# A hybrid diffusion step on one core: RWKV chunk steps with merged elementwise instructions, a planner that counts changes of first partition, and decays formed earlier

## The chip, the cores and the metric

The kernel runs on one core of a Trainium2 chip. The metric is the device time of one execution in microseconds (us). Of the core's engines five appear here: TensorE (PE; its weight loads are PEld), VectorE (DVE), ScalarE (ACT), GpSimd (POOL) and SyncE (SP, which issues all DMAs).

## The reference

Two layers work on 128 context tokens and 512 latent tokens of width 2048. Each layer normalizes and modulates its input, multiplies it by one input projection (2048 by 7056), runs three mixers on groups of the columns (gated linear attention with 6 heads, a chunked spatial MLP with 4 groups, and RWKV-7 with 12 heads), gates each and multiplies by one output projection (2048 by 2048). What the change touches is RWKV-7, a recurrence of a 64 by 64 state per head, run forwards and backwards:

```
def _rwkv7_scan(r, w, k, v, a, b, s0):
    def step(s, inp):
        r_t, w_t, k_t, v_t, a_t, b_t = inp
        sa = jnp.einsum('bhvk,bhk->bhv', s, a_t)
        s = (s * w_t[:, :, None, :] + sa[..., None] * b_t[:, :, None, :]
             + v_t[..., None] * k_t[:, :, None, :])
        return s, jnp.einsum('bhvk,bhk->bhv', s, r_t)
...
decay = jnp.exp(-jnp.exp(w_log)).reshape(N_DIR, B, L, RW_HEADS, RW_HEAD_DIM)
...
k_dir = k[None] * (1.0 + (iclr - 1.0) * lw['rw_ka'].astype(f32).reshape(hn))
b_dir = kk[None] * iclr
y_f, s_f = _rwkv7_scan(r, decay[0], k_dir[0], v, -kk, b_dir[0], s0[:, 0])
y_b, s_b = _rwkv7_scan(flip(r), flip(decay[1]), flip(k_dir[1]), flip(v), flip(-kk), flip(b_dir[1]), s0[:, 1])
```

## The kernel before

**The large products.** Every weight block is loaded in float32 (tile `raw`), split into a rounded part `whi` (ACT or DVE) and a rest `wlo` (DVE), and multiplied with the split activations `hi` and `lo` in three passes. For the input projection the 640 tokens are two halves of 320, so PE's rows read `pz<-hi,whi`, `pz<-lo,whi`, `pz<-hi,wlo` with 320 columns. The output projection has 512 columns. The modulation weights (`raw`, `csp`) are 32-wide products.

**RWKV.** `rwkv_quad` (line 895) takes four heads (two pairs, index `j`, two heads of a pair on partitions 0 to 63 and 64 to 127, index `q`) and one half of 320 tokens in each direction (index `d`), five chunks of 64. There are three quads with two halves each, six such halves in a layer and twelve in the kernel, each in this order:

- decays (lines 906 to 988), four times, once for each `j` and `d`: products with the low-rank weights (`pl<-ta,w2a`), tanh, a scan and three exponentials, then products by VectorE on one half of the partitions at a time into `ag` and `bk`, then `pl<-ag,bk` on PE, masked back into `gb` and `ag`, and transposes (`pl<-kc,bk`) into `ken`.
- inversion (lines 990 to 1050): a triangular system of 32 by 32 blocks, 31 pairs of VectorE instructions on `svu` and `lk`, and small products.
- five chunk steps (from line 1075). Each is a chain: ACT scales the state into `s0p` (eight instructions of 64 by 64); PE multiplies (`pl<-svu,ag`, 16 products into PSUM tiles X and Y); DVE copies `xs`; PE multiplies (`pl<-xs,gb`); DVE copies into `svu` (four instructions of 64 by 128); PE multiplies (`pl<-svu,ken` and `pl<-svu,gb`); DVE forms the next state with eight instructions of 64 by 64, each state times decay plus `s0p`, into `svu`, into `scar` for the next half or into `so` for the output; ACT copies the outputs into `ag`.

`rwkv_end` (line 1194) later normalizes and gates a pair's result (`pl<-kc,tw`, `pl<-tw,kc`).

**What sets the order.** The code is only recorded. `Scheduler.run` (line 300) then plays all instructions through a list of costs (`price`, line 215) and writes a fixed order for each engine; on the chip every engine follows its order and waits by semaphores. An instruction's priority is its place in the recording less a boost. RWKV has one boost, weight loads ten, the projections none: projections are what PE does while the chain of RWKV is not ready. Priorities also order who gets a buffer first; the PSUM pool `pl` has three banks for X, Y, the low-rank products and the rest of RWKV. In costs, DVE and ACT instructions follow one another with no gap:

```
            o.cost = 0.066 + 0.062 * ex + n * (0.00104 if two or ps else 0.00052)
...
                o.start = s
                t[e] = s + c
```

`layer` (line 1518) lists steps of the projections and of the other mixers; after each it records one step of RWKV (`RSTEP = 1`), once three steps of the pairs it needs are recorded. `rwkv_all` (line 1178) runs the halves one after the other: a half is recorded wholly before the next begins.

## Time and profile before

| | |
|---|---|
| median of 3 runs | 3136.03 us (3131.77 to 3136.59) |
| the profiled execution's own time | 3133.72 us |
| its span, first to last instruction | 3131.9 us |
| busy: PE, PEld, DVE, ACT, POOL | 2898.4, 2559.2, 2150.3, 1197.9, 105.0 us |
| mean granted clock of TensorE | 0.974 of full speed |

Busy time is the time in which at least one instruction of the engine runs. PE's matmuls overlap one another, so PE can be busy and still be slowed a little. A wait in the trace is idle time of an engine, put down to the instruction that released it. All instructions carry line 462 (473 in the changed program), where the order is written out; rows are told apart by the names of their tiles, and `tsm` is in these rows the small tiles, the decays `p5` among them.

### The profile page before, as it was taken

The numbers are of one execution on the slowest core, as the hardware profiler recorded it, in microseconds if no ns is written. First come the engines' busy times: TensorE is split into PE (matmuls) and PEld (weight loads), VectorE is DVE, ScalarE is ACT, GpSimd is POOL, SyncE is SP. The second block draws the span as 40 slices with busy tenths as digits, with TensorE's granted clock in tenths as the row PEclk, the third lists the DMA queues.
The fourth block names the chain that finished last, engine by engine and source line by source line (L and its number), as shares of the span: only waits on it lengthen the run. The fifth ranks groups of instructions, "written<-read, shape, count | busy, mean of one in ns | idle before, by whom it ended". The sixth has DMA issues, their size and how long they took to land. (4 is left out here: it accounts for less than half of the span.)

```text
span 3131.9 us, 64037 instructions
## 1 busy us (share of the span) xinstructions
PE 2898.4 (93%) x24531; PEld 2559.2 (82%) x24531; DVE 2150.3 (69%) x5200; ACT 1197.9 (38%) x2641; POOL 105.0 (3%) x281
## 2 busy tenths in 40 slices
PE   4899999999899999999999999999989998998998
PEld 2688688788888878988879877888879887998786
DVE  3357686785776867655576668769778696866557
ACT  3252643435343354431015336344534335434001
POOL 0000000000000000000000000000000000000000
PEclk9899899999999999999999999999999999999999
DMA  9856375565555645465463654635534453437335
GB/s 307 261 157 170 92 203 142 160 182 155 148 142 161 182 118 150 124 206 161 125 201 104 176 140 139 186 95 137 156 98 121 107 155 96 103 99 228 114 111 194
DMA packets 672154, 478.13 MB, mean 153 GB/s; under 512 B 188596, under 2 KB 606088, under 8 KB 671848
## 3 DMA queue, kind: packets, MB, share of 16 engines
q1 hardware_dynamic: 671848, 474.04, 53.3%
q8 instruction: 194, 3.18, 0.4%
q14 instruction: 112, 0.92, 0.1%
HBM read 393.63 MB, written 79.59 MB: 151 GB/s over the span
## 5 line engine op out<-in xcount | busy, mean ns | idle before, releaser
L462 PE MATMUL pz<-hi,whi 128*128 128x320 f32 (+1 forms) x3504 | 902.2, 320 | 21.4 <-ACT t L462 14.3
L462 PE MATMUL pz<-lo,whi 128*128 128x320 f32 (+1 forms) x3504 | 890.2, 316 | 0.0
L462 PE MATMUL pz<-hi,wlo 128*128 128x320 f32 (+1 forms) x3504 | 881.2, 316 | 1.6 <-DVE wlo L462 1.6
L462 PEld LDWEIGHTS pz<-hi,whi 128*128 128x128 f32 (+1 forms) x3504 | 602.9, 189 | 50.2 <-ACT t L462 19.4
L462 PEld LDWEIGHTS pz<-lo,whi 128*128 128x128 f32 (+1 forms) x3504 | 602.7, 188 | 16.6 <-issue 7.2
L462 PEld LDWEIGHTS pz<-hi,wlo 128*128 128x128 f32 (+1 forms) x3504 | 600.1, 188 | 16.8 <-issue 6.9
L462 DVE TENSOR_TENSOR wlo<-raw,whi 128x512 fp32r<-128x512 f32 (+1 forms) x640 | 435.4, 681 | 223.8 <-ACT whi L462 198.5
L462 ACT ACTIVATE whi<-raw 128x512 fp32r<-128x512 f32 (+1 forms) x445 | 277.2, 623 | 770.6 <-PE pz L462 513.1
L462 PE MATMUL pl<-ag,bk 128*128 128x128 f32 x960 | 137.7, 291 | 48.7 <-DVE bk L462 33.5
L462 DVE CAST whi<-raw 128x512 fp32r<-128x512 f32 x195 | 81.8, 421 | 141.9 <-PE pz L462 56.8
L462 PEld LDWEIGHTS pl<-ag,bk 128*128 128x128 f32 x960 | 120.6, 198 | 70.4 <-issue 59.5
L462 ACT ACT_TABLE_LOAD x124 | 159.1, 1283 | 13.5 <-DMA t<-gl 8.9
L462 ACT ACTIVATE s0p<-svu,tsm 64x64 f32<-64x64 f32 x432 | 148.0, 345 | 5.8 <-POOL svu L462 0.3
L462 DVE TENSOR_TENSOR svu<-lk,svu 104x31 f32<-104x31 f32 (+15 forms) x372 | 125.9, 339 | 18.8 <-DMA lk<-nsc 11.6
L462 DVE TENSOR_TENSOR svu<-svu 104x31 f32<-104x31 f32 (+15 forms) x372 | 126.1, 339 | 7.4
L462 DVE SCALAR_TENSOR_TENSOR svu<-pl,tsm,s0p 64x64 f32<-64x64 f32 x336 | 95.1, 283 | 41.8 <-PE pl L462 33.5
L462 ACT ACTIVATE tw<-tw 128x320 f32<-128x320 f32 (+1 forms) x180 | 76.4, 448 | 108.6 <-DVE tw L462 104.8
L462 PE MATMUL pz<-whi,hi 128*128 128x512 f32 x288 | 113.3, 394 | 1.6 <-DVE whi L462 1.5
L462 PE MATMUL pz<-wlo,hi 128*128 128x512 f32 x288 | 111.9, 393 | 2.6 <-DVE wlo L462 2.5
L462 PE MATMUL pz<-whi,lo 128*128 128x512 f32 x288 | 112.2, 391 | 0.0
L462 DVE TENSOR_TENSOR ag<-win,tw 64x320 f32<-64x320 f32 x192 | 89.3, 483 | 29.3 <-DMA yd<-ag 13.8
L462 DVE TENSOR_TENSOR gb<-pl,kc 64x384 f32<-64x384 f32 x192 | 93.0, 484 | 22.7 <-PE pl L462 20.8
(241 smaller groups left out, 4119.9 us busy)
## 6 DMA issues: line engine op xcount, KB each, us to landing
raw<-in_w_in SPq DMA_DIRECT2D x440, 256.0 KB
raw<-in_w_mod SPq DMA_DIRECT2D x256, 256.0 KB
raw<-in_w_out SPq DMA_DIRECT2D x192, 256.0 KB
win<-kr SPq DMA_DIRECT2D x48, 480.0 KB
mraw<-in_w_mod SPq DMA_DIRECT2D x85, 256.0 KB
kr<-t SPq DMA_DIRECT2D x36, 320.0 KB
t<-od SPq DMA_DIRECT2D x32, 320.0 KB
vg<-t SPq DMA_DIRECT2D x24, 320.0 KB
```

What stands on the lines that cost most here:

```text
L462: getattr(self.real[o.eng], o.fn)(*o.args, **o.kw)
```

## The change

Three things are changed.

First, in a chunk step: ACT copies the state into `s0p` without a scale, two instructions of 64 by 256 where both directions go on, and DVE adds Y to `s0p` in one instruction of 128 by 256 and multiplies by the decay, broadcast along the row, in one for each `q` (or one in all into `scar`). The four copies into `svu` become two. `at_pos` makes the access patterns over `j` and `d`. The small tiles get a pool of their own for RWKV (`tsr`, four buffers).

Second, the planner adds `DRAIN` (0.115 for DVE, 0.12 for ACT, in the planner's us) where an output starts on another partition than the output before it on that engine, and among ready instructions within 24 places of the first it prefers one with the same first partition. The cost of the 32-wide products goes from 0.111 to 0.16 for 256 columns.

Third, `rwkv_quad` yields after the low-rank products, scan and exponentials of its first `j` and `d`, and `rwkv_all` records that part of the next half after the fourth of five chunk steps (`AHEAD = 8`). Up to nine steps of RWKV are recorded after each step of the projections (`RSTEP = 9`).

The core of the diff:

```
-RSTEP = 1
+DRAIN = {"DVE": 0.115, "ACT": 0.12}
+NEAR = 24
+RSTEP = 9
+AHEAD = 8
...
+        (pitch, _), off = wr[0].ap[0], int(wr[0].offset)
+        o.part = off // int(pitch) if eng in DRAIN and pitch else 0
...
-                o.cost = 0.03 if K <= 32 else 0.111 * N / 256
+                o.cost = 0.03 if K <= 32 else 0.16 * N / 256
...
-            if e == "ACT":
-
-                i = take(a, min(range(len(a)), key=lambda j: (a[j][0] + (TABW if ops[a[j][1]].tab not in (None, table) else 0))))
+            if e in DRAIN:
+
+                p = a[0][0]
+                i = take(a, min(range(len(a)), key=lambda j: (a[j][0] > p + NEAR, ops[a[j][1]].part != part[e], a[j][0])))
...
+                if e in DRAIN:
+                    if o.part != part[e]:
+                        s = max(s, drain[e])
+                    part[e], drain[e] = o.part, s + x + c + DRAIN[e]
...
-    tsm = pool("tsm", 7)
+    tsm = pool("tsm", 5)
+    tsr = pool("tsr", 4)
...
-    scar = [[cst.tile([128, 64], F32, name=f"scar{j}{d}") for d in range(2)] for j in range(2)]
+    scar = cst.tile([128, 2, 2, 64], F32, name="scar")
...
+    def at_pos(a, strides):
+
+        return bass.AP(tensor=a.tensor, offset=a.offset, ap=[a.ap[0]] + [[s, 2] for s in strides] + list(a.ap[1:]))
...
+                if (j, d) == (0, 0):
+                    yield
...
-            for d, j, q in four:
-                if goes[d]:
-                    S.activation(out=s0p[hq[q], j, d], in_=svu[hq[q], j, d, q, pos(d, k), :], func=AF.Copy, scale=sc(d, j, q))
+            for q in range(2):
+                if both:
+                    S.copy(out=s0p[hq[q]], in_=at_pos(svu[hq[q], 0, 0, q, pos(0, k), :], (1280, 640 + 64 * (4 - 2 * k))))
...
-            for d in range(2):
-                for q in range(2):
-                    V.tensor_copy(out=svu[hq[q], :, d, q, pos(d, k), :], in_=X[hq[q], 1, :, d])
+            for q in range(2):
+                V.tensor_copy(out=at_pos(svu[hq[q], 0, 0, q, pos(0, k), :], (1280, 640 + 64 * (4 - 2 * k))), in_=X[hq[q], 1])
...
+            if both:
+                V.tensor_tensor(out=s0p, in0=Y[:, 0], in1=s0p, op=ALU.add)
+                pk = lambda r: at_pos(p5[r, pos(0, k):pos(0, k) + 1].to_broadcast([r.stop - r.start, 64]), (10, 9 - 2 * k))
+                if goes[0] == goes[1] == "carry":
+                    V.tensor_tensor(out=scar, in0=s0p, in1=pk(slice(0, 128)), op=ALU.mult)
+                elif goes[0] == goes[1] == "next":
+                    for q in range(2):
+                        V.tensor_tensor(out=at_pos(svu[hq[q], 0, 0, q, pos(0, k + 1), :], (1280, 640 + 64 * (2 - 2 * k))),
+                                        in0=s0p[hq[q]], in1=pk(hq[q]), op=ALU.mult)
...
-                        V.scalar_tensor_tensor(out=dst, in0=Y[hq[q], 0, j, d], scalar=sc(d, j, q), in1=s0p[hq[q], j, d], op0=ALU.mult, op1=ALU.add)
...
+        gens = [rwkv_quad(l, P, w, sts) for P, w in quads]
...
+                if n == AHEAD and i + 1 < len(quads):
+
+                    yield 2 * quads[i + 1][0] + 1
+                    next(gens[i + 1])
```

What this makes of the order is shown at three places, all in the third half of the second layer (the first half of its second quad) or just behind it.

VectorE in a chunk step, from one copy `xs` to the next; before:

```order
L462 COPY xs<-pl 128x256
L462 COPY svu<-pl 64x2x64 x4
L462 TENSOR_TENSOR wlo<-raw,whi 128x512
L462 SCALAR_TENSOR_TENSOR svu<-pl,tsm,s0p 64x64 x8
L462 COPY xs<-pl 128x256
```

and in the change:

```order
L473 COPY xs<-pl 128x256
L473 TENSOR_TENSOR wlo<-raw,whi 128x512
L473 COPY svu<-pl 64x2x2x64 x2
L473 TENSOR_TENSOR s0p<-pl,s0p 128x256
L473 TENSOR_TENSOR svu<-s0p,tsr 64x2x2x64 x2
L473 TENSOR_TENSOR wlo<-raw,whi 128x512
L473 COPY xs<-pl 128x256
```

Twelve instructions of the step have become five.

TensorE in the chunk steps, where the next half's low-rank products stand (`pl<-ta,w2a`, the ones that open its decays); before, between the first and the second product of the fifth step:

```order
L462 MATMUL pl<-svu,ag 64x64 x16
L462 MATMUL pl<-ta_126,w2a_4506 128x320 x2
L462 MATMUL pz<-hi,whi 128x320 x2
L462 MATMUL pz<-lo,whi 128x320 x2
L462 MATMUL pz<-hi,wlo 128x320 x2
L462 MATMUL pz<-hi,whi 128x320
L462 MATMUL pl<-ta_127,w2a_4506 128x320 x2
L462 MATMUL pz<-hi,whi 128x320
L462 MATMUL pz<-lo,whi 128x320 x2
L462 MATMUL pl<-xs,gb 64x64 x8
```

and in the change, between the second step and the third:

```order
L473 MATMUL pl<-ta_129,w2a_4145 128x320 x2
L473 MATMUL pz<-hi,whi 128x320
L473 MATMUL pz<-lo,whi 128x320 x2
L473 MATMUL pz<-hi,wlo 128x320 x2
L473 MATMUL pz<-hi,whi 128x320 x2
L473 MATMUL pl<-ta_130,w2a_4145 128x320 x2
L473 MATMUL pz<-lo,whi 128x320 x2
L473 MATMUL pl<-kc,tsr 64x64 x4
L473 MATMUL pz<-hi,wlo 128x320 x2
L473 MATMUL pz<-hi,whi 128x320 x2
L473 MATMUL pz<-lo,whi 128x320 x2
L473 MATMUL pl<-svu,ag 64x64 x16
```

They now stand ahead of the second or third step of all ten halves that have a next one; before, two or four stood ahead of the fifth in six of these, and behind all steps in the others.

VectorE at the start of a half's decays, where products on one half of the partitions follow one another (two for each of `ag` with the first exponential, `ag` with the second, and `bk` twice); before, with 4512 and 4514 the two exponentials:

```order
L462 TENSOR_TENSOR ag<-win,tw_4512 64x5x64 x2
L462 TENSOR_TENSOR ag<-win,tw_4514 64x5x64
L462 SCALAR_TENSOR_TENSOR win<-tw_4515,win 128x320
L462 TENSOR_TENSOR ag<-win,tw_4514 64x5x64
L462 TENSOR_SCALAR tw_4515<-tw_4515,pd_131 128x320
L462 SCALAR_TENSOR_TENSOR bk<-win,tw_4513 64x5x64
L462 TENSOR_TENSOR win<-tw_4515,win 128x320
L462 SCALAR_TENSOR_TENSOR bk<-win,tw_4513 64x5x64
```

and in the change, with 4151 and 4153:

```order
L473 TENSOR_TENSOR ag<-win,tw_4151 64x5x64
L473 TENSOR_TENSOR ag<-win,tw_4153 64x5x64
L473 TENSOR_TENSOR ag<-win,tw_4151 64x5x64
L473 TENSOR_TENSOR ag<-win,tw_4153 64x5x64
L473 SCALAR_TENSOR_TENSOR win<-tw_4154,win 128x320
L473 TENSOR_SCALAR tw_4154<-tw_4154,pd_134 128x320
L473 SCALAR_TENSOR_TENSOR bk<-win,tw_4152 64x5x64
L473 TENSOR_TENSOR win<-tw_4154,win 128x320
```

The four products into `ag` went 0, 64, 0, 64 by first partition, with one on all partitions between; now they go 0, 0, 64, 64.

Counted over the two built orders: PE has the same 19,037 instructions in both, SP the same 2,522. DVE has 5,190 before and 4,827 now, ACT 2,583 and 2,278 (of these table loads 124 and 134). The first partition of the output differs from that of the instruction before it at 1,572 places of DVE's order before and 891 now, on ACT at 726 and 333. Of the 1,572, 956 lie outside the stretches of chunk steps (from a half's first `xs` to its fifth) and 608 within; now 653 and 236.

## Rows read from the trace of the kernel before

**Rows 1.** The page's head and its busy times.

```profile
span 3131.9 us, 64037 instructions
PE 2898.4 (93%) x24531; PEld 2559.2 (82%) x24531; DVE 2150.3 (69%) x5200; ACT 1197.9 (38%) x2641; POOL 105.0 (3%) x281
```

**Rows 2.** Busy time by stage: a half's decays, one of twelve windows, and their sum.

```profile
core 0: us, PE busy (x) PEld busy (x) DVE busy (x) ACT busy (x) POOL busy (x), PEclk, DMA share, GB/s
2287.20:2366.60 79.40, 68.18 (x528) 63.61 (x527) 63.49 (x148) 30.90 (x75) 7.52 (x18) 0.96 0.42 109
sum 975.60, PE 911.40 PEld 843.90 DVE 759.12 ACT 404.02 POOL 66.26; mean PE 75.95 PEld 70.32 DVE 63.26 ACT 33.67 POOL 5.52
```

**Rows 3.** The same for the twelve inversions.

```profile
sum 784.60, PE 731.85 PEld 657.67 DVE 592.27 ACT 350.47 POOL 15.34; mean PE 60.99 PEld 54.81 DVE 49.36 ACT 29.21 POOL 1.28
```

**Rows 4.** The same for the twelve stretches of five chunk steps.

```profile
sum 597.90, PE 572.88 PEld 493.81 DVE 359.37 ACT 289.00 POOL 2.63; mean PE 47.74 PEld 41.15 DVE 29.95 ACT 24.08 POOL 0.22
```

**Rows 5.** Who PE waited for, 300 to 1400 us: total us, times, longest.

```profile
PE pl L462 <- DVE tw L462: 14.2, 15, 2.3
PE pz L462 <- ACT t L462: 11.2, 9, 2.6
PE pl L462 <- DVE bk L462: 10.6, 14, 2.3
PE pl L462 <- DVE ag L462: 9.3, 13, 1.9
```

**Rows 6.** The same, 1700 to 2910 us.

```profile
PE pl L462 <- DVE tw L462: 22.5, 18, 3.1
PE pl L462 <- DVE bk L462: 19.2, 12, 7.3
PE pl L462 <- DVE ag L462: 6.0, 9, 1.1
```

**Rows 7.** Timeline, 2330 to 2347 us: PE's longest wait in the second layer.

```profile
2346.01 1.41 PE L462 MATMUL pl<-ag,bk 128*128 128x128 f32 x5 [7.31 <-DVE bk L462]
```

**Rows 8.** Timeline of DVE: start us, us, instruction, count, idle before with its releaser.

```profile
2495.26 0.83 DVE L462 TENSOR_TENSOR_SCAN tw<-kc,tw 128x325 f32<-128x325 f32 x1
2496.00 0.67 DVE L462 TENSOR_TENSOR wlo<-raw,whi 128x512 fp32r<-128x512 f32 x1
...
2630.18 2.45 DVE L462 SCALAR_TENSOR_TENSOR svu<-pl,tsm,s0p 64x64 f32<-64x64 f32 x8
...
2636.53 1.24 DVE L462 COPY svu<-pl 64x128 f32<-64x128 f32 x4
```

**Rows 9.** Instructions by form: count | busy us, mean ns | idle before, releasers.

```profile
L462 ACT ACTIVATE s0p<-svu,tsm 64x64 f32<-64x64 f32 x432 | 148.0, 345 | 5.8 <-POOL svu L462 0.3
L462 DVE SCALAR_TENSOR_TENSOR svu<-pl,tsm,s0p 64x64 f32<-64x64 f32 x336 | 95.1, 283 | 41.8 <-PE pl L462 33.5
L462 DVE SCALAR_TENSOR_TENSOR scar<-pl,tsm,s0p 64x64 f32<-64x64 f32 x48 | 13.6, 283 | 3.3 <-PE pl L462 2.4
L462 DVE SCALAR_TENSOR_TENSOR tsm<-pl,tsm,s0p 64x64 f32<-64x64 f32 x48 | 13.6, 283 | 10.1 <-PE pl L462 8.9
L462 DVE COPY svu<-pl 64x128 f32<-64x128 f32 x240 | 68.9, 287 | 54.9 <-PE pl L462 32.1 <-ACT s0p L462 7.4 <-ACT whi L462 5.5
L462 DVE COPY xs<-pl 128x256 f32<-128x256 f32 x60 | 25.4, 423 | 15.8 <-PE pl L462 14.6
L462 DVE TENSOR_TENSOR md<-md,pm 128x256 f32<-128x256 f32 x32 | 13.4, 418 | 15.2 <-PE pm L462 14.9
L462 ACT COPY ss<-pm 64x256 f32<-64x256 f32 x48 | 17.6, 367 | 6.9 <-PE pm L462 6.3
L462 ACT COPY gb<-tw 32x320 f32<-32x320 f32 x96 | 43.7, 455 | 19.7 <-DMA tw<-wd 18.0
L462 ACT ACT_TABLE_LOAD x124 | 159.1, 1283 | 13.5 <-DMA t<-gl 8.9 <-DVE lo L462 1.2 <-PEq L1677 0.7
```

**Rows 10.** Timeline of PE: second low-rank product of a half, within the fifth step.

```profile
2289.95 0.56 PE L462 MATMUL pl<-ta,w2a 128*128 128x320 f32 x2 [1.21 <-ACT tw L462]
```

More of the change, by code (lines that the diff above doesn't have):

```diff
@@ L74 @@
     __slots__ = ("idx", "eng", "fn", "args", "kw", "cost", "tail", "mode", "work", "lock", "succ", "npred", "ready", "prio",
-                 "tiles", "first", "start", "end", "tab", "alts", "gang")
+                 "tiles", "first", "start", "end", "tab", "alts", "gang", "part")
 class Scheduler:
@@ L314, in run @@
         window, work, fast = 0, 0.0, True
+        part, drain = dict.fromkeys(engs, 0), dict.fromkeys(engs, 0.0)
         left = dict(self.users)
@@ L1077, in rwkv_quad @@
             goes = [end[d].get(k, "next") for d in range(2)]
+            both = all(goes)
             s0p = ts2.tile([128, 2, 2, 64], F32, tag="s0p", name="s0p")
-            sc = lambda d, j, q: p5[hq[q], 10 * j + 5 * d + pos(d, k):10 * j + 5 * d + pos(d, k) + 1]
-            for d, j, q in four:
-                if goes[d]:
-                    S.activation(out=s0p[hq[q], j, d], in_=svu[hq[q], j, d, q, pos(d, k), :], func=AF.Copy, scale=sc(d, j, q))
+            for q in range(2):
+                if both:
+                    S.copy(out=s0p[hq[q]], in_=at_pos(svu[hq[q], 0, 0, q, pos(0, k), :], (1280, 640 + 64 * (4 - 2 * k))))
+                else:
+                    for d in range(2):
+                        if goes[d]:
+                            S.copy(out=s0p[hq[q], :, d], in_=svu[hq[q], :, d, q, pos(d, k), :])
             with together():
@@ L1101, in rwkv_quad @@
                     mm(Y[hq[q], 1, j, d], gb[hq[q], j, d, pos(d, k), 64:128], svu[hq[q], j, d, q, pos(d, k), :], start=False)
[L1102 to L1110 removed]
+            if both:
[7 more added lines that the diff above has]
+                                        in0=s0p[hq[q]], in1=pk(hq[q]), op=ALU.mult)
+            else:
+                for d in range(2):
+                    if goes[d]:
+                        V.tensor_tensor(out=s0p[:, :, d], in0=Y[:, 0, :, d], in1=s0p[:, :, d], op=ALU.add)
@@ new lines, in rwkv_quad @@
+            for d in range(2):
+                if not goes[d] or both and goes[0] == goes[1]:
+                    continue
+                pj = lambda r: at_pos(p5[r, 5 * d + pos(d, k):5 * d + pos(d, k) + 1].to_broadcast([r.stop - r.start, 64]), (10,))
+                if goes[d] == "next":
+                    for q in range(2):
+                        V.tensor_tensor(out=svu[hq[q], :, d, q, pos(d, k + 1), :], in0=s0p[hq[q], :, d], in1=pj(hq[q]), op=ALU.mult)
+                elif goes[d] == "carry":
+                    V.tensor_tensor(out=scar[:, :, d], in0=s0p[:, :, d], in1=pj(slice(0, 128)), op=ALU.mult)
+                else:
+                    for j, p in enumerate(ps2):
+                        so = TR()
+                        V.tensor_scalar(out=so, in0=s0p[:, j, d], scalar1=p5[:, 10 * j + 5 * d + pos(d, k):10 * j + 5 * d + pos(d, k) + 1],
+                                        scalar2=None, op0=ALU.mult)
@@ L1180, in rwkv_all @@
         late = []
-        for P in range(pairs // 2):
-            for w in range(2):
-                for n, _ in enumerate(rwkv_quad(l, P, w, sts)):
-                    if n == 4 and w == 0:
-                        while late:
-                            rwkv_end(l, *late.pop(0))
-                    yield 2 * P + 1
-            late += [(2 * P, sts[2 * P]), (2 * P + 1, sts[2 * P + 1])]
-            yield min(2 * P + 3, pairs - 1)
+        quads = [(P, w) for P in range(pairs // 2) for w in range(2)]
+        gens = [rwkv_quad(l, P, w, sts) for P, w in quads]
+        for i, (P, w) in enumerate(quads):
+            if i == 0:
+                next(gens[0])
+                yield 1
+            n = 0
+            for _ in gens[i]:
+                n += 1
+                if n == 4 and w == 0:
+                    while late:
+                        rwkv_end(l, *late.pop(0))
+                yield 2 * P + 1
+                if n == AHEAD and i + 1 < len(quads):
+                    yield 2 * quads[i + 1][0] + 1
+                    next(gens[i + 1])
+            if w:
+                late += [(2 * P, sts[2 * P]), (2 * P + 1, sts[2 * P + 1])]
+            if i + 1 < len(quads):
+                yield 2 * quads[i + 1][0] + 1
+        yield -1
         while late:
@@ L1558, in layer @@
             for _ in range(RSTEP):
-                if not rdone and cnt.get(need, 0) >= 3:
+                if not rdone and (cnt.get(need, 0) >= 3 if need >= 0 else cnt.get(pairs - 1, 0) >= 4):
                     rstep()
```

24 lines of the change are left out of this document (10 added, 14 removed).

## The prediction

> **What bounds the kernel now.** I read the page's busy times first [rows 1]: PE is busy for 2898.4 of 3131.9 us, and the built order gives it the same instructions after the change, in nearly the same number of groups. So nothing here shortens PE's work. What can be gained is PE's waiting, at most the 3131.9 - 2898.4 = 233.5 us in which it is idle, and a large part of that is the start of the program, which the change leaves alone.
>
> Next I cut the two layers into the stages of RWKV, since PE fills every stage with projections, and asked for the busy time of each engine in each [rows 2 to 4]. PE is idle for 975.6 - 911.4 = 64.2 us beside the decays, 784.6 - 731.9 = 52.7 us beside the inversions and 597.9 - 572.9 = 25.0 us beside the chunk steps. That is 142 us in all. DVE is busy for 78%, 75% and 60% of these stages: it is the second engine, and the fuller it is the more PE waits. The steps, which most of the diff is about, are where PE waits least.
>
> Then the waits themselves [rows 5, 6]. Six rows on DVE carry 14.2 + 10.6 + 9.3 + 22.5 + 19.2 + 6.0 = 81.8 us: matmuls that need `bk`, `ag` or the `tw` of `rwkv_end`. One row on ACT, where a `pz` bank waits to be emptied, carries 11.2 us. The longest wait [rows 7] shows the kind: PE's order is fixed, the product of `ag` and `bk` stood at its head, DVE was 7.31 us late with `bk`, and every projection behind it stood still. PE had work; the plan had put it in the wrong place, since it thought DVE would be sooner.
>
> Why DVE is later than planned can be seen in its timeline [rows 8]. The scan on all partitions takes 0.83 us and the next instruction, also on all, starts 0.74 us after it, 0.09 us ahead of its end. Eight instructions of 0.283 us [rows 9] that alternate between partitions 0 and 64 take 2.45 us, so they start (2.45 - 0.283) / 7 = 0.310 us apart, 0.027 us after the end of the one before. A change of first partition thus costs 0.117 us that the plan before does not have. The Trainium skill says the same in other words (VectorE: DVE Perf Modes, section Two Vector instructions with no wait between them): an instruction is held until all earlier ones have finished if the quadrant of an input or of the output differs from the last one in that memory; this trace agrees, with 0.027 us behind the end against 0.09 ahead of it. Its section The DRAIN you can't avoid says that every instruction waits for an empty pipe; by that, regrouping saves nothing and only the number of instructions counts, which is the third case below.
>
> **The change part by part.** *Regrouping, and a plan that counts it.* The changes of partition outside the steps fall from 956 to 653. Before, 956 x 0.117 = 112 us of DVE's time in 975.6 + 784.6 = 1760 us of decays and inversions were not in the plan; PE is idle there for 117 us, so the lateness is of the size of the waits. Now 36 us of it are gone and the other 76 us are in the plan, so that PE's order leaves room for them. Not every wait is of this kind: what the plan misses in DMA landings, semaphores and ACT stays. The ends are nothing and all of the six rows, -81.8 us. I take half, -41 us: a wait of 7.31 us is more than the changes of partition ahead of it can explain alone, and many of the short ones are less.
>
> *Merged instructions on DVE.* Removed are 95.1 + 13.6 + 13.6 + 68.9 = 191.2 us [rows 9]. Added are 120 copies of 64 by 256 at the price of `xs` (0.423 us, 50.8 us), 48 sums of 128 by 256 and 72 products of 64 by 256 at that of `md` (0.418 us, 50.2 us), six into `scar` (2.5 us) and 60 smaller ones at no more than 0.287 us (17.2 us): 120.7 us, so 70 us less work, most of it in the steps. In the chain of one step eight instructions of 2.45 us become three of about 1.3 us, and four copies of 1.24 us [rows 8] two of 0.87 us: 1.5 us shorter, 90 us over 60 steps. But PE has projections to do meanwhile. It pays only where PE waits, and that is 25.0 us in all steps. The ends are 0 and -25 us; I take a third, -8 us, since part of that idle time is turning between products of different shapes, which stays.
>
> *Merged instructions on ACT.* 432 scalings, 148.0 us, become 96 copies of 64 by 256, priced between the copy from PSUM (0.367 us) and the wider one from SBUF (0.455 us), and 24 smaller ones: some 47 us. Against this stand ten more table loads in the built order, 10 x 1.283 = 13 us [rows 9]. ACT is 41% busy in the decays and 48% in the steps [rows 2, 4], so neither is on the path by itself; with some 88 us less to do it empties `pz` sooner. Of the 11.2 us [rows 5] I take a third, -4 us, between 0 and all.
>
> *The next half's first decays beside the steps.* Its four products, two tanh, a scan and three exponentials are only moved. DVE and ACT have room there (60% and 48%). What is new is that they stand in PE's order and in the pool of three `pl` banks ahead of the third step's products in all ten halves, where six had two or four of them ahead of the fifth. In one of those six PE waited 1.21 us for the bank that ACT's tanh frees [rows 10], with the chain's `xs` product behind it. Four more halves at 1.21 us are +5 us. The ends are 0, if ACT, with two copies in place of eight scalings, is in time, and the price of the slower case below. The gain from products that can start sooner is in the first term.
>
> *The rest.* Nine steps recorded at once and a pool of its own for small tiles change only who comes first among instructions of the same boost; the 32-wide products cost more in the plan and the same on the chip. I price them at nothing. They lie among the projections, which cover them, and without that cover a wait for weights would show; it is inside the range.
>
> The sum is -41 - 8 - 4 + 5 = -48 us. It is made against the profiled execution's 3133.7 us, 2.3 us below the median of the runs; so 3136.0 - 48 = **3088 us**.
>
> **The rivals.** *First, the plan was late for this reason alone.* Then all six rows go, -82 us, half of the steps' idle time, -12 us, half of ACT's, -6 us, and +5 us stays: -95 us, **3041 us**. For it speaks that 112 us not planned and 117 us idle are so close; against it, that the longest waits are longer than the changes ahead of them.
>
> *Second, the lead-in turns into a wait, and the kernel is slower.* PE stands at a product with the low-rank weights until a bank is free, ACT comes to the tanh only after its own work and one more table load, and the step's `xs` product waits behind in PE's order. With two products in each half, each at the 1.21 us seen plus a load of 1.28 us, that is 5 us in each of ten halves, +50 us. It decides if it meets all ten and the plan's better timing gives half of what I took, -24 us: +26 us, **3162 us**. For it speaks the wait that exists, and the ten loads; against it, that ACT loses two thirds of its work on `s0p`, which stood in front of that tanh.
>
> *Third, the change does not do what the planner says.* If regrouping bought nothing (the page's rule on draining, or a lateness that has other causes), the six rows stay and only merging counts: -8 + 5 = -3 us, **3133 us**, no change. The timeline speaks against it with its 0.117 us.
>
> **How the numbers follow.** About 0.2%, 6.3 us, is what a measurement of this kernel can tell from no change. The forecast has a chance of 0.62, the first rival 0.15, the second 0.13 and the third 0.10. So faster by more than that has 0.62 + 0.15 = 0.77, within it 0.10, slower 0.13. The forecast's own range is 3050 to 3125 us. For 8 times in 10 the range goes down to 3040, half of the first rival, and up to 3135, through the third; beyond lie the slower case and the other half of the first.
>
> **What would show it.** Right: the rows of PE waiting for DVE `bk`, `ag` and `tw` halve in both layers; PE's idle time falls beside decays and inversions more than beside steps; DVE's busy time falls by 70 us and ACT's by about 88. Single steps would be wrong if the waits for DVE stay as they are while DVE's instructions overlap more (third rival), or if PE waits for ACT `tw` at `pl<-ta,w2a` for 20 us or more (second rival). The whole would be wrong if PE's idle time in the stages stays at 140 us, or if its busy time grows by a lower granted clock.

## The result: 3094.3 us, 1.2% faster, and the profile after

The changed kernel takes 3094.31 us (median of 4 runs, 3090.82 to 3102.59) against 3134.84 us for the kernel before: a ratio of 0.9876, with 0.9854 to 0.9897 as its 95% interval. That is 40.5 us less, where 48 were forecast. The page's head and busy times after answer to [rows 1]:

```profile
span 3091.8 us, 63438 instructions
PE 2864.1 (93%) x24531; PEld 2540.9 (82%) x24531; DVE 2068.5 (67%) x4837; ACT 1097.7 (36%) x2336; POOL 104.7 (3%) x281
```

DVE has 82 us less to do and ACT 100 us less. The surprise is PE: with the same 24531 products it is busy for 34.3 us less, while its idle time only goes from 233.5 to 227.7 us. The mean granted clock hardly moved (0.974 and 0.973).

**The stages.** In the changed kernel the first decays of a half stand beside the steps of the half before, so I cut the decays here from the last product of the half before. By this cut the kernel before has, for its twelve decays:

```profile
sum 941.80, PE 882.65 PEld 819.21 DVE 744.79 ACT 372.65 POOL 72.03; mean PE 73.55 PEld 68.27 DVE 62.07 ACT 31.05 POOL 6.00
```

And after, decays, inversions and steps, the last two beside [rows 3] and [rows 4]:

```profile
sum 942.30, PE 904.27 PEld 850.35 DVE 730.97 ACT 378.87 POOL 74.01; mean PE 75.36 PEld 70.86 DVE 60.91 ACT 31.57 POOL 6.17
sum 780.90, PE 713.31 PEld 642.09 DVE 580.50 ACT 314.26 POOL 12.62; mean PE 59.44 PEld 53.51 DVE 48.37 ACT 26.19 POOL 1.05
sum 562.60, PE 554.90 PEld 483.96 DVE 308.23 ACT 226.19 POOL 2.95; mean PE 46.24 PEld 40.33 DVE 25.69 ACT 18.85 POOL 0.25
```

PE's idle time goes from 59.2 to 38.0 us beside the decays and from 25.0 to 7.7 us in the steps, but from 52.7 to 67.6 us beside the inversions. The decays are as long as before, yet PE does 21.6 us more in them. So lengths alone mislead: a stage that is longer may hold more projections. The 14.9 us that the inversions lose come mostly with the planner's part: in the run **plan** below PE is idle beside them for 71.2 us, in **merge** for 60.1. What makes them longer there was not looked into.

**Lengths with the projections they hold.** The next view is the same one of windows, for the instructions of tile `pz` alone. The windows are the first layer's RWKV, the stretch up to the second layer's, the second layer's, and what lies behind its last step; the number behind "x" counts the projection products. Before:

```profile
174.30:1354.70 1180.40, 788.14 (x4769) 0.98 0.55 151
1354.70:1696.00 341.30, 187.97 (x890) 0.98 0.54 163
1696.00:2839.90 1143.90, 806.32 (x4936) 0.98 0.48 130
2839.90:3131.90 292.00, 147.09 (x655) 0.97 0.54 169
```

After:

```profile
175.90:1322.50 1146.60, 781.82 (x4780) 0.98 0.56 156
1322.50:1664.50 342.00, 187.77 (x890) 0.99 0.54 162
1664.50:2803.70 1139.20, 822.88 (x5065) 0.98 0.49 133
2803.70:3091.80 288.10, 127.50 (x526) 0.92 0.51 162
```

The first layer is 33.8 us shorter with 11 more products. The second is only 4.7 us shorter, but holds 129 more. Behind its last step there are 129 fewer, and that stretch is only 3.9 us shorter, with the granted clock down from 0.97 to 0.92. For the price of such a product I take the row of a run further down, in which this last stretch holds 405 instead of 655: (147.09 - 103.51) / 250 = 0.174 us. So the two layers gained 33.8 + 4.7 + 140 x 0.174 = 62.9 us, and behind them 129 x 0.174 - 3.9 = 18.5 us were lost. I call these the net times of a stretch; they are an estimate. Most of the 250 products have 320 columns and 27 have 512; by the first layer's own mean, 788.14 / 4769 = 0.165 us, they shift by up to some 3 us.

**The waits.** After, PE's waits in the body (300 to 2875 us; engine and what it waited for, total us, times, longest), beside [rows 5, 6]:

```profile
PE pl L473 <- DVE tw L473: 45.6, 32, 6.8
PE pz L473 <- ACT t L473: 10.7, 8, 2.0
PE pl L473 <- DVE bk L473: 10.4, 12, 2.5
PE pl L473 <- DVE gb L473: 10.1, 17, 1.6
```

`bk` and `ag` together had 45.1 us [rows 5, 6]; `bk` has 10.4 now and `ag` no longer appears among the rows of a few us. A wait for `gb` came up, 10.1 us. The one for `tw` did not halve but grew. [rows 5, 6] leave out 1400 to 1700 us; over the whole body, 300 to 2910 us, it was before

```profile
PE pl L462 <- DVE tw L462: 38.1, 35, 3.1
```

The 7.5 us more are those behind the second layer's last step, where `tw` had 9.7 us and has 17.6 (below). The groups of products on which these waits fall show it in one place (busy us, mean ns of one, idle time before them with its releasers). Before:

```profile
L462 PE MATMUL pl<-ag,bk 128*128 128x128 f32 x960 | 137.7, 291 | 48.7 <-DVE bk L462 33.5 <-DVE ag L462 14.5
L462 PE MATMUL pl<-kc,bk 128*128 128x128 f32 x240 | 44.2, 282 | 1.2 <-DVE ag L462 0.8
L462 PE MATMUL pl<-tw,kc 128*128 128x256 f32 (+1 forms) x72 | 22.5, 395 | 24.3 <-DVE tw L462 24.1
L462 PE MATMUL pl<-kc,tw 128*128 128x128 f32 x60 | 14.0, 301 | 13.0 <-DVE tw L462 12.2 <-PE pz L462 0.4 <-issue 0.4
```

After:

```profile
L473 PE MATMUL pl<-ag,bk 128*128 128x128 f32 x960 | 132.5, 284 | 23.3 <-DVE bk L473 12.1 <-DVE gb L473 9.4 <-DVE ag L473 1.1
L473 PE MATMUL pl<-kc,bk 128*128 128x128 f32 x240 | 36.3, 274 | 1.1 <-DVE gb L473 1.1
L473 PE MATMUL pl<-tw,kc 128*128 128x256 f32 (+1 forms) x72 | 24.6, 428 | 32.8 <-DVE tw L473 29.9 <-DVE tsr L473 2.7
L473 PE MATMUL pl<-kc,tw 128*128 128x128 f32 x60 | 16.6, 342 | 21.2 <-DVE tw L473 13.9 <-DMA xag<-xr_d 7.3
```

The first row is the decays: 25.4 us of idle time gone. The last two are `rwkv_end`, the ends of the pairs: 37.3 us became 54.0. Most of the growth lies in the first 65 us behind the second layer's last step, where no chain of steps is left and few projections are. All engines there (columns as in [rows 2]), before and then after:

```profile
2839.90:2904.90 65.00, 52.07 (x312) 46.31 (x308) 43.14 (x105) 26.70 (x52) 0.00 (x0) 0.92 0.88 275
```

```profile
2803.70:2868.70 65.00, 38.00 (x185) 30.13 (x182) 41.33 (x101) 18.17 (x36) 0.00 (x0) 0.74 0.81 247
```

```profile
PE pl L473 <- DVE tw L473: 17.6, 5, 6.8
PE pl L473 <- DMA xag<-xr_d: 7.3, 1, 7.3
```

PE is idle there for 27.0 us instead of 12.9, nearly all in those two waits, and a mean granted clock of 0.74 means that about half of the stretch ran at the lower level of 1.2 GHz instead of 2.4. TensorE was busy all of the first 11.3 us, with a clock of 1.00; from 2835 to 2855 us, behind the first long wait, it was busy for 2.7 of 20 us, with a clock of 0.50.

**The merged instructions** cost what was forecast:

```profile
L473 ACT COPY s0p<-svu 64x256 f32<-64x256 f32 x96 | 38.6, 402 | 9.2 <-DVE svu L473 6.8 <-DVE modt L473 0.8
L473 DVE COPY svu<-pl 64x256 f32<-64x256 f32 x120 | 50.6, 422 | 68.5 <-PE pl L473 61.3 <-issue 2.2 <-ACT whi L473 1.9
L473 DVE TENSOR_TENSOR svu<-s0p,tsr 64x256 f32<-64x256 f32 x72 | 30.2, 419 | 1.9
L473 DVE TENSOR_TENSOR s0p<-pl,s0p 128x256 f32<-128x256 f32 x48 | 20.4, 425 | 38.5 <-PE pl L473 38.2
```

0.422, 0.419 and 0.425 us stand against the 0.423 and 0.418 us taken from `xs` and `md` [rows 9].

### The profile page after: what moved, and what is told of

The parts are those of the page before. It is cut to its first block, busy times and chain, and to the rows that moved or that the text cites. A ratio compares the mean times of both kernels' runs of the same rounds, so it can differ in the third digit from the quotient of the medians.

```text
span 3091.8 us, 63438 instructions
## 1 busy us (share of the span) xinstructions
PE 2864.1 (93%) x24531; PEld 2540.9 (82%) x24531; DVE 2068.5 (67%) x4837; ACT 1097.7 (36%) x2336; POOL 104.7 (3%) x281
## 4 chain that ended last, share of the span: by engine, by line
PE 53%; DMA 19%; DVE 17%; SPq 4%; issue 3%; ACT 3%; DVEq 0%; ACTq 0%; POOL 0%; POOLq 0%
PE pz L473 31%; PE pl L473 15%; PE pm L473 7%; DMA raw<-in_w_in 4%; SPq L473 4%; DVE svu L473 4%; DVE wlo L473 3%; DVE tw L473 2%; DMA mraw<-in_w_mod 2%; DVE t L473 2%; DMA tw<-yd 2%; DVE ag L473 2%; ACT whi L473 1%; DMA raw<-in_w_mod 1%; DVE gb L473 1%
## 5 line engine op out<-in xcount | busy, mean ns | idle before, releaser
L473 PEld LDWEIGHTS pz<-hi,whi 128*128 128x128 f32 (+1 forms) x3504 | 600.3, 188 | 43.7 <-ACT t L473 14.1
L473 PE MATMUL pl<-ag,bk 128*128 128x128 f32 x960 | 132.5, 284 | 23.3 <-DVE bk L473 12.1
L473 DVE TENSOR_TENSOR gb<-pl,kc 64x384 f32<-64x384 f32 x192 | 93.2, 485 | 18.8 <-PE pl L473 16.3
L473 DVE TENSOR_TENSOR ag<-win,tw 64x320 f32<-64x320 f32 x192 | 86.2, 483 | 27.2 <-DMA yd<-ag 14.9
L473 DVE COPY svu<-pl 64x256 f32<-64x256 f32 x120 | 50.6, 422 | 68.5 <-PE pl L473 61.3
L473 DVE TENSOR_TENSOR ag<-pl,kc 64x384 f32<-64x384 f32 x192 | 89.8, 484 | 6.0 <-PE pl L473 4.7
```

Of the source, the lines that this page charges most:

```text
L473: getattr(self.real[o.eng], o.fn)(*o.args, **o.kw)
```

## The experiments

All numbers stand against the kernel before, run on the same chip. The net times and the idle times are from one profiled execution each, and such an execution scatters: three kernels below with the same 4780 projections in the first layer had it 33.8, 21.9 and 21.7 us shorter. Net times are trusted to about 12 us, ratios to their intervals. The profiled executions of defer and merge_load took 14 us more than their medians and that of lead 5 us less, so the net gains of the first two look too small here. "Ends" is the idle time of PE before the products of `rwkv_end`, "ag, bk" that before `pl<-ag,bk`.

| kernel | median us | ratio (95%) | net, two layers | net, outside | idle: ag, bk | idle: ends |
|---|---|---|---|---|---|---|
| before | | 1 | | | 48.7 | 37.3 |
| plan | 3127.11 | 0.9973 (0.9961 to 0.9984) | -49.1 | +42.2 | 27.1 | 74.6 |
| merge | 3105.12 | 0.9912 (0.9895 to 0.9930) | -30.2 | +1.6 | 36.1 | 35.7 |
| lead | 3151.53 | 1.0061 (1.0041 to 1.0081) | -7.8 | +20.3 | 39.7 | 53.2 |
| merge_plan | 3090.39 | 0.9861 (0.9842 to 0.9881) | -59.5 | +12.8 | 32.3 | 54.5 |
| merge_lead | 3095.21 | 0.9873 (0.9853 to 0.9892) | -36.7 | -0.9 | 41.8 | 34.7 |
| whole change | 3094.31 | 0.9876 (0.9854 to 0.9897) | -62.9 | +22.8 | 23.3 | 54.0 |
| nonear | 3109.55 | 0.9912 (0.9892 to 0.9933) | -41.0 | +20.0 | 30.0 | 53.4 |
| defer | 3095.15 | 0.9875 (0.9854 to 0.9896) | -47.9 | +23.4 | 27.7 | 53.4 |
| defer_twin | 3079.02 | 0.9808 (0.9785 to 0.9831) | -58.9 | +8.5 | 20.7 | 45.2 |
| merge_load | 3099.73 | 0.9897 (0.9879 to 0.9915) | -19.2 | -1.0 | 38.2 | 37.2 |
| merge_act8 | 3083.19 | 0.9836 (0.9823 to 0.9850) | -41.7 | -8.8 | 29.5 | 34.4 |
| mp_twin | 3103.70 | 0.9886 (0.9867 to 0.9904) | -46.2 | +16.3 | 32.8 | 57.8 |
| ml_twin | 3090.54 | 0.9858 (0.9840 to 0.9877) | -32.8 | -2.6 | 43.4 | 34.0 |

### One part at a time

**plan**: the planner's part alone; the steps stay as in the kernel before.

```diff
+DRAIN = {"DVE": 0.115, "ACT": 0.12}
+NEAR = 24
...
+                i = take(a, min(range(len(a)), key=lambda j: (a[j][0] > p + NEAR, ops[a[j][1]].part != part[e], a[j][0])))
...
+                        s = max(s, drain[e])
...
+                o.cost = 0.03 if K <= 32 else 0.16 * N / 256
```

> Only the planner is changed (changes of first partition counted and avoided, the new cost of the 32-wide products); chunk steps, recording order and pools are those of before. Theory A (PE waited because DVE's and ACT's changes of partition were not in the plan): the waits for bk and ag in decays fall to a third, and most of the 40 us comes from here: 3135 - 28 = 3107 us. Theory B (less work on DVE and ACT is what counts): within 6 us of before, 3130 to 3140 us. Theory C (the earlier start of the next half's decays counts): no change either.

Measured: 0.9973, 7.9 us faster by the medians, far from what theory A wanted. The idle time before `pl<-ag,bk` fell from 48.7 to 27.1 us, not to a third. Yet the view of the projections says that A's mechanism worked in part (the same four windows):

```profile
174.20:1351.00 1176.80, 799.41 (x4877) 0.98 0.55 153
1351.00:1689.80 338.80, 168.94 (x784) 0.96 0.52 160
1689.80:2850.50 1160.70, 836.93 (x5186) 0.98 0.50 135
2850.50:3125.00 274.50, 103.51 (x405) 0.90 0.49 152
```

In the two layers 358 more projections were done while the layers became 13.2 us longer: 358 x 0.174 - 13.2 = 49.1 us net. But the stretch between the layers lacks 106 products and is shorter by only 2.5 us, and the last one lacks 250, worth 43.5 us, and is shorter by 17.5. There PE waits for the ends of the pairs. By group over the whole span, and by wait in the 65 us behind the last step:

```profile
L472 PE MATMUL pl<-ag,bk 128*128 128x128 f32 x960 | 131.8, 284 | 27.1 <-DVE bk L472 15.3 <-DVE gb L472 10.1 <-POOL t L472 0.9
...
L472 PE MATMUL pl<-tw,kc 128*128 128x256 f32 (+1 forms) x72 | 26.7, 460 | 33.0 <-DVE tw L472 32.8 <-ACT ag L472 0.2
L472 PE MATMUL pl<-kc,tw 128*128 128x128 f32 x60 | 16.2, 345 | 41.6 <-DVE tw L472 25.6 <-ACT tsm L472 13.5 <-issue 1.6
```

```profile
PE pl L472 <- DVE tw L472: 20.5, 7, 7.7
PE pl L472 <- ACT tsm L472: 13.5, 1, 13.5
```

21.6 us of idle time are gone from `pl<-ag,bk`, and 37.3 us are added at the ends. The gain in the layers was given back behind them. The reading that fits is that the projections that the better plan brings forward are the ones that used to cover `rwkv_end`; *The ends of the pairs* below sets the runs side by side for it.

**merge**: the merged instructions of the steps alone (`DRAIN = {}`, `RSTEP = 1`, no early decays).

```diff
-                    S.activation(out=s0p[hq[q], j, d], in_=svu[hq[q], j, d, q, pos(d, k), :], func=AF.Copy, scale=sc(d, j, q))
+                    S.copy(out=s0p[hq[q]], in_=at_pos(svu[hq[q], 0, 0, q, pos(0, k), :], (1280, 640 + 64 * (4 - 2 * k))))
...
+                V.tensor_tensor(out=s0p, in0=Y[:, 0], in1=s0p, op=ALU.add)
```

> Only the chunk steps are changed (merged instructions); the planner's costs, the recording order and the pools are those of before. Theory A: 8 us less, since PE waits only 25 us in the steps, 3127 us, and the waits for bk and ag stay at about 45 us. Theory B: most of the gain, 25 us or more, 3110 us or less, with PE's idle time in the steps near 8 us. Theory C: under 8 us.

Measured: 0.9912, 29.9 us faster by the medians, more than twice what my sum gave the merged instructions. The five-step stretches are 48.1 us shorter in all than [rows 4]:

```profile
sum 549.80, PE 532.81 PEld 459.70 DVE 314.26 ACT 230.84 POOL 4.31; mean PE 44.40 PEld 38.31 DVE 26.19 ACT 19.24 POOL 0.36
```

They hold 183 fewer projections, though, worth 31.8 us; net the steps gain 16.3 us and the decays 17.7 by the same count, and the inversions lose 3.8. The time is what theory B had, but PE's idle time in the steps is 17.0 us and not near 8. The ends are as before (35.7 us of idle time), so nothing is given back there.

**lead**: the recording alone.

```diff
+RSTEP = 9
+AHEAD = 8
...
+                if (j, d) == (0, 0):
+                    yield
...
+                if n == AHEAD and i + 1 < len(quads):
```

> Only the recording is changed (first decays of the next half beside the steps, up to nine steps recorded at once, own pool for the small tiles); planner and chunk steps are those of before. Theory A: 0 to 5 us more, 3135 to 3140 us, with waits of PE for the bank that the tanh frees. Theory B: no change. Theory C: 15 us or more less, 3120 us or less, since the first product of a half's ag and bk comes some 5 us sooner after the steps.

Measured: 1.0061, 16.5 us slower, where the sum had +5. It is not the wait that the second rival named: over the body (300 to 2930 us) PE waits 3.5 us for ACT's `tw`; before, 300 to 2910 us, it was 5.1. The view of the projections, second layer and what lies behind it:

```profile
1685.60:2864.20 1178.60, 837.37 (x5138) 0.98 0.48 131
2864.20:3144.40 280.20, 114.61 (x453) 0.92 0.49 155
```

It moves 202 projections of the second layer forward and gets nothing for them there (34.7 us longer, net -0.4 us in that layer); behind the last step the ends wait (23.2 us for DVE `tw` and 7.2 for ACT `tsr` in the first 65 us), and the 65 us have a granted clock of 0.71.

### Two parts at a time

**merge_plan** and **merge_lead** each leave out one part of the change: the first keeps `RSTEP = 1` and the old recording, the second `DRAIN = {}` and the old price of the 32-wide products.

> Merged chunk steps and the changed planner, the recording of before. Theory A: the sum of the two alone, 3135 - 28 - 8 = 3099 us, within 6 us of the whole change. Theory B: the same as merging alone, 3110 us or less. Theory C: 15 us or more behind the whole change, 3110 us or more.

> Merged chunk steps and the changed recording; the planner's costs are those of before. If the three parts add up (merging -28 us, recording +17 us as they measured alone), 3135 - 28 + 17 = 3124 us, with waits of PE for the products of the pairs' ends of 60 us or more. If the merged steps take away what made the changed recording slow (ACT with eight scalings in front of the tanh), 3105 us, the same as merging alone.

Measured: 0.9861 and 0.9873. On top of the merging the planner's part is worth 0.9861 against 0.9912, some 15 us; that is 9 us below the sum of theory A. The recording turns from a loss into a gain, 0.9873 against 0.9912, some 10 us, more than either theory had; its ends wait for 34.7 us instead of 53.2. With both the whole change has 0.9876, no better than with one of the two. Its net time in the layers is the best of all in the table, 62.9 us, but defer, with as many projections in each layer, has 47.9; it loses 22.8 us outside them. The parts don't add up. That they draw on the same projections fits this and is not shown by itself.

**nonear**: the whole change, but the planner takes by priority alone, so that changes of partition are counted and not avoided.

```diff
-                i = take(a, min(range(len(a)), key=lambda j: (a[j][0] > p + NEAR, ops[a[j][1]].part != part[e], a[j][0])))
+                i = take(a, min(range(len(a)), key=lambda j: a[j][0]))
```

> The whole change, but the planner only counts a change of first partition and takes ready instructions by priority alone, as before. Theory A (what pays in the planner's part is that it counts them): within 8 us of the whole change, 3087 to 3103 us, with more changes of partition on DVE. Theory D (what pays is that there are fewer of them): 12 us or more slower than the whole change, 3106 us or more.

Measured: 0.9912, 15 us slower than the whole change and, on the same chip, 14 us slower than merge_lead, which has no planner's part at all. In its built order the first partition changes at 1,128 places on DVE and 420 on ACT; merge_lead has 1,124 and 415, the whole change 891 and 333. Its net gain in the layers is near that of merge_lead (41.0 and 36.7 us), and its loss outside them is that of the whole change (20.0 and 22.8 us). So counting without avoiding bought nothing in this order, as theory D has it. It is one order, and two orders can lie 20 us apart for reasons that stay open (merge_act8 below), so that the fewer changes are what pays is likely and not shown.

### The ends of the pairs

The 7.3 us wait for a DMA behind the last step and the waits for `tw` suggested two causes: `rwkv_end`'s loads queue behind other loads, or the chain of its six pieces is held by its few buffers. A third stands in the runs above: there is too little left to do meanwhile. PE's idle time in the first 65 us behind the last step goes with the number of projections that are left from there on: 34.7 us with 405 (plan), 30.8 with 453 (lead), 27.0 with 526 (whole change), 19.0 with 587 (merge_plan), 15.3 with 649 (merge_lead), 12.9 with 655 (before) and 9.4 with 683 (merge).

**defer**: the whole change, with the loads of the output projection's residual rows recorded in the middle of its 16 blocks and not ahead of them.

```diff
-                y = ys[t] = x_tile(*t)
-                Q.dma_start(out=y, in_=x_src(l, *t))
             for n, k in enumerate(KORD):
+                if n == 8:
+                    for t in tiles:
+                        y = ys[t] = x_tile(*t)
+                        Q.dma_start(out=y, in_=x_src(l, *t))
```

> The whole change, and in the output projection the loads of the residual rows are recorded after eight of the sixteen blocks in place of ahead of the first. Theory E (at the end of the second layer the pairs' last loads stand behind the output projection's loads in the DMA queues, and PE behind them): the 25 us that PE waits for them behind the last step fall to 15 us or less, and the time by 8 to 15 us, to about 3083 us. Rival F (the pairs' end is a chain through its seven buffers, whatever else is loaded): within 4 us of the whole change, 3090 to 3098 us.

Measured: 0.9875, no difference from the whole change. The DMA's wait is gone, and the wait for DVE behind it took its place, 24.6 us where 17.6 + 7.3 = 24.9 stood:

```profile
PE pl L473 <- DVE tw L473: 24.6, 7, 6.7
```

**defer_twin**: the same, and half of the pieces of the last two pairs are loaded into the two `twin` buffers, which are free by then.

```diff
-            rwkv_end(l, *late.pop(0))
+            rwkv_end(l, *late.pop(0), alt=(2,) if len(late) else (0, 4))
...
-                    x = W3()[:, 0:nw]
+                    x = room.pop(0) if room else W3()[:, 0:nw]
```

> As the run before, and every second piece of the last two pairs' ends is loaded into the two window buffers that are idle by then, so that two pieces can be under way at once. Theory E: nothing more than the later loads alone, about 3083 us. Rival F: the waits behind the last step fall to 10 us or less and the time to about 3070 us.

Measured: 0.9808 (0.9785 to 0.9831), the fastest kernel of all: by the medians 56 us under the kernel before and, on the same chip, 16 us under defer. The first 65 us behind the last step, and the largest waits in them:

```profile
2791.80:2856.80 65.00, 49.03 (x289) 43.49 (x286) 42.31 (x107) 23.89 (x46) 0.00 (x0) 0.92 0.89 268
```

```profile
PE pl L473 <- DVE win L473: 7.0, 3, 5.2
PE pl L473 <- DVE tw L473: 3.2, 2, 2.1
```

PE's idle time there goes from 27.0 to 16.0 us and the granted clock from 0.74 back to 0.92. Theory E, the queue, doesn't fit; theory F, the chain through the buffers, had 3070 us. The new order also keeps 94 more projections for the last stretch (620 against 526). From 526 to 655 of them the idle time falls by 27.0 - 12.9 = 14.1 us, so by this estimate the 94 alone are worth 10 us of the 11 to 12 that went. Buffers and cover are not told apart by this run.

**mp_twin** and **ml_twin** make the same edit of the buffers, without the deferred loads, in merge_plan and merge_lead.

> Merged chunk steps and the changed planner with the recording of before, and every second piece of the last two pairs' ends loaded into the idle window buffers; the residual rows are loaded where they were. Rival F, which held: the 20 us of waits for the pairs' products behind the second layer's last step fall below 8 us, and the time from 3090 to about 3077 us. If the later loads of the residual rows were needed as well: 3088 us or more.

> Merged chunk steps and the changed recording without the planner's part, with the same loading of the last pairs' ends. The waits behind the second layer's last step are 14 us without it; by Rival F half of that goes, 3095 - 8 = 3087 us. If this beats the run above, the planner's part buys nothing once the pairs' ends are not in its way.

Measured: 0.9886 against 0.9861 without it, slower if anything, and 0.9858 against 0.9873, within the intervals. In mp_twin the waits moved to the new tile: PE is idle for 26.2 us before the products of `win`, and 57.8 us in all before the ends against 54.5. With the same number of projections left, the idle time in the first 65 us goes from 19.0 to 24.2 us in mp_twin and from 15.3 to 8.9 in ml_twin. So the edit of the buffers is no sure gain in itself. mp_twin's time is also what its expectation gives for the case that the later loads are needed as well; the buffers without the later loads were not run in the whole change, so this stays open. And ml_twin beats mp_twin, which the second expectation names as the sign that the planner's part buys nothing once the ends are out of its way; the intervals overlap, so the runs neither show that nor rule it out.

### Shorter chain or less work

**merge_load** adds to merge six sums of 64 by 64 on alternating partitions in each step, without a boost; nothing uses their results.

```diff
+            keep, sch.boost = sch.boost, 0
+            for n in range(6):
+                V.tensor_tensor(out=scr[hq[n % 2]], in0=xs[hq[n % 2], n % 2, n // 3], in1=kc[hq[n % 2], 64:128], op=ALU.add)
+            sch.boost = keep
```

**merge_act8** keeps the merged DVE instructions and gives ACT its eight copies of 64 by 64 back, without the scale.

```diff
-                    S.copy(out=s0p[hq[q]], in_=at_pos(svu[hq[q], 0, 0, q, pos(0, k), :], (1280, 640 + 64 * (4 - 2 * k))))
+            for d, j, q in four:
+                if goes[d]:
+                    S.copy(out=s0p[hq[q], j, d], in_=svu[hq[q], j, d, q, pos(d, k), :])
```

> Merged chunk steps alone, and beside each step six instructions of VectorE on 64 by 64 that alternate between partitions 0 and 64 and whose results nobody uses: with 60 x 6 of them at some 0.31 us, 112 us, DVE is as much occupied as before the merging (70 us of work and 372 changes of partition at 0.117 us went), but the chain of a step stays as short as merged. Theory G (the shorter chain is what pays): 3105 to 3115 us, near merging alone at 3105 us. Theory H (the time that DVE gets free for the weights' split and the pairs' ends pays): 3120 to 3135 us.

> Merged chunk steps alone, but ACT copies the state in eight instructions of 64 by 64 again, as many as before. If VectorE's part carries the gain of 30 us: 3102 to 3112 us. If ACT's part does (the copies into svu wait for the eight readings of the state, and the splits of the weights queue behind them): 3120 to 3135 us.

Measured: 0.9897 and 0.9836, neither slower than merge. The added sums and the stretches of steps in merge_load:

```profile
L472 DVE TENSOR_TENSOR scr<-xs,kc 64x64 f32<-64x64 f32 x360 | 79.1, 220 | 10.5
```

```profile
sum 552.60, PE 534.76 PEld 459.63 DVE 380.17 ACT 225.97 POOL 4.32; mean PE 44.56 PEld 38.30 DVE 31.68 ACT 18.83 POOL 0.36
```

DVE is busier in the steps than before the change (380.2 against 359.4 us in [rows 4]), and the steps are still 45.3 us shorter. They hold 223 fewer projections, so net they gain only 6.4 us, in an execution that took 14 us more than the median. What decides is the time: 3099.73 us is beyond theory G's range on the fast side and 20 us below theory H's. DVE's freed time (theory H) is not needed for the gain; that the shorter chain pays (theory G) is what is left of the two. The copies of merge_act8:

```profile
L472 ACT COPY s0p<-svu 64x64 f32<-64x64 f32 x432 | 103.5, 242 | 23.3 <-DVE svu L472 14.4 <-POOL svu L472 2.9 <-DVE tsm L472 0.8
```

In merge the wider copies in their place take 38.7 us, and the 24 narrower ones 7.1; 58 us more of ACT's work cost nothing. That it is 22 us faster than merge I can't explain in full: its granted clock is 0.980 against 0.975, so (3103.3 x 0.025 - 3081.4 x 0.020) x 2 = 32 us fewer ran at half the clock, and a us at half clock costs at most half a us, 16 us. Why this order keeps the clock up better stays open. It shows how far two orders of the same products can lie apart.

## Why the prediction was right, and where its steps were wrong

The time, 3094.3 us, is 6 us from the forecast and in its own range. The steps behind it held less well than that.

**The bound on what can be gained** failed. I wrote that nothing shortens PE's work and that only its 233.5 us of idle time could be won. Idle time fell by 5.8 us and busy time by 34.3 us, with the same products at the same mean clock. By group the rows above have 7.9 us less at `pl<-kc,bk` and 5.2 at `pl<-ag,bk`, and many others have less too; a group's busy time includes what other groups overlap, so these are no shares of the 34.3 us. The gain at `pl<-kc,bk` comes in with the planner's part (36.5 us in plan, 44.0 in merge). Since the ends of matmuls are modelled, a product that starts a little late can look like a longer product; that this is what fell is argued and not shown.

**The planner's part, -41 us**, is the step that was mis-sized: alone it measured -7.9 us, and some -15 on top of the merging. Its mechanism held in the layers: 49.1 us net, and the idle time before `pl<-ag,bk` fell by about the half that I took (48.7 to 27.1 us in plan, 23.3 in the whole change). Two things in the step were wrong. I put the waits for `tw` in with the others as one kind, 36.7 of the 81.8 us; they belong to `rwkv_end`, and over the body they grew from 38.1 to 45.6 us. And I priced at nothing what the projections cover once they are gone from behind the layers: 42 us in plan. The profile before had the row for it, a wait for `tw` of 22.5 us in the second layer [rows 6].

**Merged instructions, -8 on DVE and -4 on ACT**, measured some -30 together. I let the shorter chain pay only where PE is idle in the steps, 25.0 us. But the steps gain 16.3 us net and the decays behind them 17.7; that a shorter step keeps its projections for a place where they cover more fits this and is argued. The prices of the instructions were right. The busy times of merge, beside [rows 1]:

```profile
PE 2881.1 (93%) x24531; PEld 2551.9 (82%) x24531; DVE 2081.0 (67%) x4835; ACT 1111.6 (36%) x2338; POOL 106.7 (3%) x281
```

DVE's fell by 69.3 us where 70 were forecast, ACT's by 86.3 where it was 88. Less work itself was not what counted, by merge_load and merge_act8.

**The recording, +5 us**, measured +16.5 alone, -10 on merge and +4 on merge_plan with intervals that overlap. The waits of the lead-in for ACT's `tw`, on which the term and the second rival rested [rows 10], came to 0.4 us in the whole change. The mechanism fell; what it does is to move projections forward, for good or ill.

**The signs.** The waits for `bk` and `ag` more than halved, those for `tw` did not. PE's idle time was to fall beside decays and inversions more than beside steps; it fell by 59.2 + 52.7 - 38.0 - 67.6 = 6.3 us beside the first two and by 17.3 beside the steps. In all three it went from 136.9 to 113.3 us, so the sign against the whole did not come.

**The rivals.** The first, that the plan was late for this reason alone, falls with plan. The second did not happen, though lead alone was slower, with longer waits at the ends. The third, that regrouping buys nothing, is not borne out: plan is faster than before beyond its interval, and nonear is slower than the whole change. Its sum leaves out the 4 us of ACT's merged instructions without a reason; with them it is -7 us, 3129 us. The section on draining that it leans on in the Trainium skill (VectorE: DVE Perf Modes, The DRAIN you can't avoid) says itself that an instruction that is not held starts earlier; the trace agrees, with a start 0.09 us ahead of the end [rows 8]. Taken in the order merging, planner, recording, the measured steps are some -30, -15 and +4 us: 26 us too much for the planner and 18 too little for the merging nearly cancel, and the recording's term is right in that order alone. So the time was right by luck, by a sum whose terms were not.

**What stays open.** The effects of the parts depend on which others are there, and the planner's order answers to any edit with 10 to 20 us: merge_load does more work than merge and is no slower, the same buffers gain in one order and not in another. An effect of a part that is under 20 us, as the planner's and the recording's on top of the merging, is therefore not told from what any new order may bring. The recording with the planner's part alone was not run, and the new price of the 32-wide products, the pool `tsr` and the nine steps recorded at once have no runs of their own. Why merge_act8 keeps a higher clock, and whether defer_twin gains by its buffers or by the projections that stay behind, is not settled.

## What to carry to other kernels

Filler work is a budget: what a better plan pulls forward beside one chain is missing as cover for the next one, so before a wait is counted as gained, look for the stretch that the fillers covered (here the ends of the last pairs, behind both layers) and price it uncovered. Compare stretches by their length together with the number of filler products in them, since length or idle time alone hides such a move. Where a planner writes the order, test the parts in combinations and expect every edit to move the time by half a per cent by itself.

## What the runs showed of the hardware

A change of partition holds an instruction on ScalarE as on VectorE. Over all neighbours in the trace of before with nothing waited for, VectorE's next instruction starts 0.080 us ahead of the end of the last without a change and 0.031 us behind it with one (medians of 2825 and 1468 pairs); ScalarE's 0.096 us ahead and 0.013 us behind (865 and 622 pairs). On VectorE another 81 pairs keep their output's partition and change that of an input, and they are held just the same, 0.031 us behind the end. The planner, which looks at outputs alone, doesn't count those. The Trainium skill states this for inputs too (VectorE: DVE Perf Modes, section Two Vector instructions with no wait between them); the trace agrees, with 0.031 us against -0.080.

A copy of 64 by 64 on ScalarE takes 0.242 us as COPY (merge_act8, above) and 0.345 us as ACTIVATE with a scale for each partition [rows 9]; what of this is the scale was not measured.

TensorE's clock is part of the price of uncovered work. In the 65 us behind the second layer's last step the mean granted clock was 0.92 with 12.9 us of idle time (before), 0.74 with 27.0 (whole change), and 0.92 again with 16.0 (defer_twin): the products that are left there run partly at 1.2 GHz instead of 2.4.
